# Two feed-forward stages: the expanding matrix products by seven block products in place of eight, with some weight rests and partial sums made by accumulating DMAs

## The chip, the cores and the metric

One core of one Trainium2 chip. The metric is device microseconds (us) from the start of the program to its end. Of the kernel before, three runs give a median of 1385.18 us (1383.61 to 1386.09).

## The reference, cut to what matters

Two transformer blocks run one after the other on 512 tokens of width 1024. Both end in a feed-forward stage, and those two stages are what changes:

```python
# block one: D_FF = 4096
def _sq_relu_mlp(h, w1, w2):
    return jnp.square(jax.nn.relu(h @ w1)) @ w2
...
# block two: D_FF_2 = 2816
x = x + ((jax.nn.silu(h2 @ w_gate[l]) * (h2 @ w_up[l])) @ w_down[l]).astype(x.dtype)
```

So there are three expanding products (w1, here `w_mlp_in`; `w_gate`; `w_up`) and two contracting ones (`w_mlp_out`, `w_down`). All inputs are float32.

## The kernel before, in words

Activations lie transposed: 128 features on the partitions, 512 tokens along the free axis, so a width of 1024 is eight tiles of 128x512.

**Products.** Every float32 matrix is split into a head and a rest in the fp32r format (`hi`, `lo`), and a product is three TensorE products: head by head, head by rest, rest by head (`mm3`, line 619). `dense_tile` (line 791) makes one output tile of 128 features by 512 tokens from all k-tiles of 128: for `w_mlp_in`, `w_gate` and `w_up` that is 8 k-tiles, 24 TensorE products, into one PSUM bank.

**Weights.** `weights` (line 610) loads up to 128x1024 float32 on SyncE's (SP's) queue into a tile of class `raw` (4 buffers), ScalarE casts it to `hi`, and VectorE subtracts to get `lo`. Head and rest take one buffer each of class `w` (10 of them). All of that is per 24 TensorE products in the expanding stages.

**The stages.** `block1` (line 847) makes in turn: the mixer, the product with `w_out`, the residual and norm that give the eight inputs `h2`, and then four parts (`FF1`). A part computes eight tiles of the hidden layer (up), squares them, splits them, and then adds its share to the eight output tiles `y` (down), which stay in SBUF; VectorE adds each part's bank to `y`. `block2` does the same with gate and up together in two parts (`FF2`, 12 and 10 tiles), adding to the residual stream `x`. Between the two parts of the program lie the mixers of block two.

**What sets the order.** The program is first recorded as a list of operations. `Plan.schedule` then issues them one at a time against a table of durations and the state of the buffers, and thereby fixes each engine's order. Nothing is decided at run time: an engine takes its instructions in this order, and each waits for its own inputs. Tile names such as `bank_4348` carry a number that grows with the order in which tiles are first used, so equal numbers on two engines are at about the same place in the program.

Of the kernel before, what the change touches and what calls it, by code (L numbers as in the profile page):

```python
# [67 lines left out]
class Tag:  # L68
    def __init__(self, cls, shape, dtype, cap=None):
        self.cls, self.shape, self.dtype, self.cap = cls, shape, dtype, cap  # L70
        self.needs = [] if cls == "fixed" else [cls] + ([cap[0]] if cap else [])
        self.users = 0
        self.writer = [None, None]
        self.readers = [[], []]
        self.slot = None
        self.real = None
        self.owner = None


class View:  # L80
# [7 lines left out]
    def rows(self, i):  # L88
        v = self[64 * i:64 * i + 64]
        v.parts = (i,)  # L90
        return v
# [89 lines left out]
class Cost:  # L181
# [3 lines left out]
    def __init__(self, eng, fn, args, kw):  # L185
# [5 lines left out]
        elif eng == "SP":  # L191
            self.time = 470
        else:
# [44 lines left out]
class Machine:  # L238
# [38 lines left out]
    def commit(self, c, op, t):  # L277
# [10 lines left out]
        if c.eng == "SP":  # L288
            self.dma = max(self.dma, t + 1150) + op.nbytes / 360.0
            return self.dma + 950  # L290
# [18 lines left out]
class Plan:  # L309
# [13 lines left out]
    def record(self, choices):  # L323
# [12 lines left out]
        op.nbytes = 4 * math.prod(out.shape) if eng == "SP" else 0  # L336
# [144 lines left out]
    def place(self, tag):  # L481
        if tag.real is None:
            self.count += 1
            n = f"{tag.cls}_{self.count}"
            if tag.slot is None:
# [9 lines left out]
    def issue(self, nc, pool, slots, banks):  # L495
        self.pool, self.slots, self.banks, self.count = pool, slots, banks, 0
# [14 lines left out]
FF1 = ((0, 8), (8, 16), (16, 24), (24, 32))  # L511
FF2 = ((0, 12), (12, 22))
SHIFT = 260
LATER = {'mem_norm': 10, 'mem_keys': 100, 'mem_values': 40, 'mod_cols': 140, 'rope_tables': -150, 'late_prologue': 0, 'pool': 90, 'weights': 10, 'lower_bound': 120, 'hgrn': 60, 'add_sq': 120, 'load_raw': 10}
# [5 lines left out]
WIDTH = {"t": 528, "raw": 1024, "w": 1024, "big": 1664, "tmp": 16}  # L520
CAPS = {'t': 54, 'raw': 4, 'w': 10, 'big': 2, 'tmp': 32, 'bank': 8}
# [15 lines left out]
class Builder:  # L537
# [22 lines left out]

    def stat_bank(self, s="st"):
# [28 lines left out]
    def weights(self, src, n, raw=None, engines=None):  # L590
        if raw is None:
            raw = self.load_raw(src, n)
        hi = self.plan.tile("w", [128, 1024], R)
        lo = self.plan.tile("w", [128, 1024], R)
        self.copy(hi[:, :n], raw[:, :n], engines or ("ACT", "POOL"))
        self.tt(ALU.subtract, lo[:, :n], raw[:, :n], hi[:, :n].bitcast(F), engines)
        return hi, lo

# [185 lines left out]
    def chunked(self, w, mt, kts, k0=0):  # L784
        out, o = [], k0
        for kt in kts:
            hi, lo = self.weights(self.a[w][mt, :, o * 128:(o + kt) * 128], kt * 128)
# [13 lines left out]
    def moving(self, w, outs, views, xs):  # L801
        n = len(xs)
        for k in range(n):
            if k % 2 == 0:
                wh, wl = self.weights(self.a[w][k // 2], 1024)
            self.moving_k(wh, wl, k % 2, outs, views, xs[k], k == 0, k == n - 1)

    def build(self):
# [5 lines left out]
        with (  # L814
            tc.tile_pool(name="fixed", bufs=1) as pool,
            tc.tile_pool(name="slots", bufs=1) as sp,
            tc.tile_pool(name="banks", bufs=1, space=PSUM) as pp,
        ):
            with tc.manual_schedule():
                self.plan.issue(nc, pool, sp, pp)  # L820
# [21 lines left out]
    def block1(self):  # L842
# [236 lines left out]
        h2 = []  # L1079
        for k in range(8):  # L1080
            self.residual(k, mo[k], ro)
            h2.append(self.apply_norm(self.x[k], 512, a2[:, k:k + 1], rb, sh2[:, k:k + 1]))
        y, acc = [], None
        self.mem_keys()
        for part, (f0, f1) in enumerate(FF1):
# [6 lines left out]
            for m in range(f0, f1):  # L1092
                b = self.bank("ff")
                self.dense_tile(b, self.chunked("w_mlp_in", m, (8,)), h2)
                r, hi, lo = self.sf("r"), self.sr("ah"), self.sr("al")
                nc.scalar.activation(r, b, AF.Relu)
                nc.scalar.activation(hi, r, AF.Square)
                sq = self.sf("r2")
                self.tt(ALU.mult, sq, r, r)
                self.sub(lo, sq, hi.bitcast(F))  # L1100
                act.append((hi, lo))
            for m in range(8):
                b = self.bank("fo")
                self.dense_tile(b, self.chunked("w_mlp_out", m, (8, 8)[:1] + (f1 - f0 - 8,) * (f1 - f0 > 8), f0), act)
                if part == 0:
                    o = self.sf("y")
                    self.copy(o, b)
                    y.append(o)
                else:
                    nc.vector.tensor_tensor(out=y[m], in0=y[m], in1=b, op=ALU.add)  # L1110
                if part == len(FF1) - 1:
                    acc = self.add_sq(acc, self.square(y[m]))
        self.tail = (y, self.bcast(self.rsqrt(self.stats([acc], 512)[:, :4], 4, 1024), 0, 512), gg2)

# [30 lines left out]
    def pool(self, g, ub):  # L1145
# [3 lines left out]
        u = self.plan.tile("t", [128, 528], F)  # L1149
# [3 lines left out]
        cur, step, n = u, 1, 528  # L1153
        while step < w:
            nxt = self.plan.tile("t", [128, 528], F)
# [136 lines left out]
    def block2(self):  # L1292
# [116 lines left out]
        h = [self.scaled(self.x[k], gn[:, k:k + 1]) for k in range(8)]  # L1409
        rw = self.wide_norm(self.sum_sq(self.x, 512), 512, 1024)  # L1410
        for part, (f0, f1) in enumerate(FF2):
            act = []
            for m in range(f0, f1):
                bg, bu = self.bank("g"), self.bank("u")
                self.dense_tile(bg, self.chunked("w_gate", m, (8,)), h)
                self.dense_tile(bu, self.chunked("w_up", m, (8,)), h)
                sg, p = self.sf("sg"), self.sf("gu")
                nc.vector.tensor_tensor(out=sg, in0=bg, in1=rw, op=ALU.mult)
                nc.scalar.activation(sg, sg, AF.Silu)
                nc.vector.tensor_tensor(out=p, in0=bu, in1=rw, op=ALU.mult)  # L1420
                self.tt(ALU.mult, p, p, sg)
                hi, lo = self.pair(512)
                self.split(p, hi, lo)
                act.append((hi, lo))
            for m in range(8):
                ch = self.chunked("w_down", m, (8, f1 - f0 - 8), f0)
                if part == 0:
# [203 lines left out]

def tile_b(w):
# [50 lines left out]
def host(i):  # L1683
# [44 lines left out]
    d["w_mlp_in"] = tile_a(i["w_mlp_in"][0])  # L1728
# [35 lines left out]
```

## Time and profile before

| | |
|---|---|
| median of the runs | 1385.18 us |
| the profiled execution | 1385.12 us |
| its span, first to last instruction | 1383.3 us |
| TensorE products busy | 1338.9 us, 97% of the span |
| VectorE busy | 846.7 us, 61% |
| ScalarE busy | 571.9 us, 41% |
| GpSimd busy | 38.6 us, 3% |
| DMA, mean | 107 GB/s |

Busy time of an engine is the union of its instructions. TensorE's instructions overlap one another, so the mean duration of one product (some 390 ns for 512 columns) is longer than the spacing from one to the next, and the spacing is what a stretch full of them costs. VectorE's instructions overlap a little at their ends too.

### The profile page before, as it was taken

Reading aid. Unit: us, or ns where it says so; the run is one execution under the profiler, and the core shown is the slowest. Engines: PE = TensorE matmul, PEld = TensorE weight load, DVE = VectorE, ACT = ScalarE, POOL = GpSimd, SP = SyncE. Lnnn points to the kernel's source line nnn. Section 1 sums busy time; section 2 is a strip of 40 time slices with the busy share of each in tenths; the row PEclk is TensorE's granted clock in tenths of the full one; section 3 lists DMA queues with packets and bytes.
Section 4 is the critical chain, followed back from the end, with each engine's and each line's share of the span. In section 5 each row is a group of like instructions: output and inputs, shape, how many; then the busy total and the mean of one; then the engine's idle time right before and its main releaser. Section 6 shows DMA issues by size and latency. Waiting matters only on the chain.

```text
span 1383.3 us, 18475 instructions
## 1 busy us (share of the span) xinstructions
PE 1338.9 (97%) x7202; PEld 1068.7 (77%) x7202; DVE 846.7 (61%) x1544; ACT 571.9 (41%) x952; POOL 38.6 (3%) x58
## 2 busy tenths in 40 slices
PE   6999999999999999999899899999999999999999
PEld 4777777867887888887688677778788888888887
DVE  5787889784453743445845879998864443344432
ACT  4444466544242332334435656667433222232220
POOL 1021120000000000000000000000000000000000
PEclk9999999999999999999899999999999999999999
DMA  9654654232542233323233020211322223332231
GB/s 343 216 138 140 207 186 136 93 105 87 183 151 76 82 102 99 100 92 92 91 91 107 17 66 25 76 46 47 122 76 101 97 69 91 115 107 91 69 101 59
DMA packets 48663, 148.47 MB, mean 107 GB/s; under 512 B 5568, under 2 KB 7232, under 8 KB 48576
## 3 DMA queue, kind: packets, MB, share of 16 engines
q1 hardware_dynamic: 48576, 147.30, 33.4%
q8 instruction: 56, 0.92, 0.3%
q14 instruction: 31, 0.25, 0.1%
HBM read 143.61 MB, written 2.10 MB: 105 GB/s over the span
## 4 chain that ended last, share of the span: by engine, by line
PE 88%; DVE 8%; DMA 2%; issue 1%; ACT 1%; SPq 0%; DVEq 0%; ACTq 0%
PE bank L508 88%; DVE t L508 5%; ACT t L508 1%; DVE tmp L508 1%; DMA raw<-w_mod_b 1%; DVE fixed L508 1%; DVE bank L508 1%; DMA t<-w_mod_a 0%; SPq L508 0%; DMA raw<-w_in_qk 0%; DVE w L508 0%; DVE big L508 0%; ACT w L508 0%; ACT tmp L508 0%; DVEq L508 0%
## 5 line engine op out<-in xcount | busy, mean ns | idle before, releaser
L508 PE MATMUL bank<-t,w 128*128 128x512 f32 (+1 forms) x4716 | 1098.6, 391 | 9.3 <-DVE w L508 4.0
L508 PEld LDWEIGHTS bank<-t,w 128*128 128x128 f32 x4716 | 867.8, 189 | 212.5 <-DVE t L508 6.7
L508 DVE TENSOR_TENSOR w<-raw,w 128x1024 fp32r<-128x1024 f32 (+2 forms) x217 | 250.3, 1158 | 391.4 <-PE bank L508 250.2
L508 ACT CAST w<-raw 128x1024 fp32r<-128x1024 f32 (+2 forms) x214 | 212.0, 994 | 420.2 <-PE bank L508 383.2
L508 DVE TENSOR_TENSOR t<-t,t 128x512 f32<-128x512 f32 (+4 forms) x286 | 167.9, 610 | 35.0 <-ACT t L508 28.0
L508 ACT ACTIVATE t<-t 128x256 f32<-128x256 f32 (+2 forms) x192 | 100.9, 543 | 47.7 <-DVE t L508 32.9
L508 PE MATMUL bank<-t,t 128*64 128x128 f32 (+5 forms) x796 | 92.8, 281 | 6.9 <-DVE t L508 4.3
L508 PEld LDWEIGHTS bank<-t,t 128*128 128x128 f32 (+2 forms) x796 | 73.9, 161 | 23.6 <-DVE t L508 7.7
L508 PE MATMUL bank<-w,t 128*128 128x512 f32 x312 | 76.1, 396 | 0.0
L508 ACT COPY t<-bank 128x512 f32<-128x512 f32 (+3 forms) x93 | 47.9, 518 | 67.7 <-PE bank L508 64.4
L508 ACT ACTIVATE t<-bank 128x512 f32<-128x512 f32 (+2 forms) x74 | 43.4, 587 | 72.6 <-PE bank L508 71.6
L508 PEld LDWEIGHTS bank<-w,t 128*128 128x128 f32 x312 | 57.8, 188 | 15.1 <-ACT t L508 1.3
L508 ACT CAST t<-t 128x512 fp32r<-128x512 f32 (+2 forms) x77 | 44.2, 584 | 55.1 <-DVE t L508 53.5
L508 DVE TENSOR_TENSOR t<-bank,t 128x512 f32<-128x512 f32 (+3 forms) x86 | 56.8, 661 | 8.6 <-PE bank L508 5.4
L508 PE MATMUL bank<-t,fixed 128*32 128x256 f32 (+3 forms) x246 | 38.5, 498 | 13.3 <-DMA t<-w_mod_a 12.3
L508 DVE SCALAR_TENSOR_TENSOR t<-raw,fixed,t 128x512 f32<-128x512 f32 x56 | 43.0, 810 | 12.3 <-DMA raw<-w_mod_b 12.2
L508 PE MATMUL bank<-fixed,t 128*128 128x128 f32 (+2 forms) x292 | 46.8, 279 | 3.4 <-ACT t L508 1.5
L508 PEld LDWEIGHTS bank<-fixed,t 128*128 128x128 f32 x292 | 35.3, 161 | 15.1 <-issue 5.2
L508 DVE TENSOR_TENSOR t<-t 128x512 f32<-128x512 f32 (+1 forms) x68 | 37.9, 557 | 4.5 <-DMA t<-xP 4.1
L508 DVE SCALAR_TENSOR_TENSOR t<-t,fixed,t 128x512 f32<-128x512 f32 (+3 forms) x60 | 38.4, 676 | 1.2 <-ACT t L508 0.9
L508 ACT ACTIVATE t<-bank,fixed 128x512 f32<-128x512 f32 (+2 forms) x32 | 21.8, 682 | 33.2 <-PE bank L508 33.0
L508 PEld LDWEIGHTS bank<-t,fixed 128*32 128x32 f32 (+1 forms) x246 | 13.6, 131 | 27.2 <-ACT fixed L508 12.3
(93 smaller groups left out, 552.8 us busy)
## 6 DMA issues: line engine op xcount, KB each, us to landing
raw<-w_mod_b SPq DMA_DIRECT2D x32, 512.0 KB, 3.9
raw<-w_mlp_in SPq DMA_DIRECT2D x32, 512.0 KB, 3.6
raw<-w_mlp_out SPq DMA_DIRECT2D x32, 512.0 KB, 3.8
raw<-w_in SPq DMA_DIRECT2D x22, 512.0 KB, 3.6
raw<-w_gate SPq DMA_DIRECT2D x22, 512.0 KB, 3.2
raw<-w_up SPq DMA_DIRECT2D x22, 512.0 KB, 3.2
t<-w_mod_a SPq DMA_DIRECT2D x32, 256.0 KB, 6.0
raw<-w_out SPq DMA_DIRECT2D x16, 512.0 KB, 3.8
```

The costliest lines, as they stand in the source:

```text
L508: getattr(engines[eng], fn)(*[real(z) for z in args], **{k: real(z) for k, z in kw.items()})
```

## The change

In the three expanding products an output of 256 features by 512 tokens is now seen as a 2x2 arrangement of blocks (two feature tiles, two halves of 256 tokens), and so is each pair of k-tiles. Seven block products of 256 columns, on sums and differences of weight blocks and of input blocks, take the place of eight. This is the Winograd form of Strassen's method.

- `tile_s` lays these weights out in blocks. `strassen_weights` loads four blocks (128x1024 float32), makes four sums on VectorE (`s1` to `s4`, 256 wide), casts three blocks and the four sums on ScalarE, and makes the two rests: that of the sums (1024 wide) on VectorE; that of the blocks (768 wide) on VectorE for `w_mlp_in`, and for `w_gate` and `w_up` by `rest_dma`: ScalarE writes minus the head, and a DMA that GpSimd issues adds the float32 weights to it from memory.
- `strassen` runs 4 x 7 x 3 = 84 products of 256 columns for two output tiles, into four banks (`quad`). `strassen_sums` puts the result together on ScalarE and VectorE (one copy, two adds of 512, three of 256), `split_quarters` splits it.
- The first two pairs of tiles in block one and the first in block two are made by the ordinary eight (`plain`), while `right_sums` makes the sums of the inputs.
- `weights_dma` loads `w_out`, `w_mem_k`, `w_mem_v` and the plain `w_mlp_in` straight into the head by a DMA that GpSimd issues, and the rest by `rest_dma`.
- The partial sums `y` of block one move to device memory: a part copies its bank and adds it there by an accumulating DMA; the last part reads them back.
- Six parts in block one, four in block two, counted in pairs of tiles. Class `w` now has 5 buffers of twice the width.

```diff
-FF1 = ((0, 8), (8, 16), (16, 24), (24, 32))
-FF2 = ((0, 12), (12, 22))
+FF1 = ((0, 3), (3, 6), (6, 9), (9, 12), (12, 14), (14, 16))
+FF2 = ((0, 3), (3, 6), (6, 9), (9, 11))
+BY_DMA = ("w_out", "w_mem_k", "w_mem_v")
+PLAIN_BY_DMA = ("w_mlp_in",)
+PLAIN1, PLAIN2 = 2, 1
+REST_BY_DMA = ("w_gate", "w_up")
...
-WIDTH = {"t": 528, "raw": 1024, "w": 1024, "big": 1664, "tmp": 16}
-CAPS = {'t': 54, 'raw': 4, 'w': 10, 'big': 2, 'tmp': 32, 'bank': 8}
+WIDTH = {"t": 512, "raw": 1024, "w": 2048, "big": 1664, "tmp": 16}
+CAPS = {'t': 56, 'raw': 4, 'w': 5, 'big': 2, 'tmp': 32, 'bank': 8}
...
+    def weights_dma(self, src, n):
+        hi, lo = self.plan.tile("w", [128, 2048], R).halves()
+        self.nc.gpsimd.dma_start(hi[:, :n], src)
+        self.rest_dma(hi[:, :n], lo[:, :n], src)
+        return hi, lo
...
+    def rest_dma(self, hi, lo, src):
+
+        self.nc.scalar.activation(lo, hi.bitcast(F), AF.Copy, scale=-1.0)
+        self.nc.gpsimd.dma_start(lo, src, accum_op=ALU.add)
...
+    def strassen_weights(self, w, m, u):
+        n, src = 256, self.a[w][m, u]
+        raw = self.load_raw(src, 4 * n)
+        a21, a11, a12, a22 = (raw[:, i * n:(i + 1) * n] for i in range(4))
+        st = self.big(1024)
+        s2, s1, s4, s3 = (st[:, i * n:(i + 1) * n] for i in range(4))
+        self.tt(ALU.subtract, s3, a21, a11)
+        self.tt(ALU.add, s1, a21, a22)
+        self.tt(ALU.add, s2, s3, a22)
+        self.tt(ALU.subtract, s4, a12, s2)
+        (ha, la), (hs, ls) = (self.plan.tile("w", [128, 2048], R).halves() for _ in range(2))
+        self.copy(ha[:, :3 * n], raw[:, n:4 * n], ("ACT",))
+        if w in REST_BY_DMA:
+            self.rest_dma(ha[:, :3 * n], la[:, :3 * n], src[:, n:4 * n])
+        else:
+            self.tt(ALU.subtract, la[:, :3 * n], raw[:, n:4 * n], ha[:, :3 * n].bitcast(F))
+        self.copy(hs, st[:, :4 * n], ("ACT",))
+        self.tt(ALU.subtract, ls, st[:, :4 * n], hs.bitcast(F))
...
+        for k in range(n):
+            for a, b, bank, half in (("a11", "b11", 0, 0), ("a12", "b21", 1, 0), ("a22", "t4", 2, 1), ("s3", "t3", 3, 0),
+                                     ("s1", "t1", 0, 1), ("s2", "t2", 1, 1), ("s4", "b22", 2, 0)):
+                out = quad[bank][:, 256 * half:256 * half + 256]
+                wh, wl = left[k][a]
+                xh, xl = xs[k][b]
+                first = k == 0 and a in ("a11", "a12", "a22", "s3")
+                for i, (w, x) in enumerate(((wh, xh), (wh, xl), (wl, xh))):
+                    t.matmul(out, w, x, start=first and i == 0, stop=k == n - 1 and i == 2, skip_group_check=True)
+        return self.strassen_sums(quad)
...
+    def strassen_sums(self, quad):
+        w, x, y, z = quad
+        s, c, v = self.sf("ps"), self.sf("cu"), self.sf("cd")
+        self.copy(s, w, ("ACT", "DVE"))
+        self.tt(ALU.add, c.rearrange("p (b w) -> p b w", b=2), x.rearrange("p (b w) -> p b w", b=2),
+                s[:, :256].rearrange("p (o w) -> p o w", o=1).to_broadcast([128, 2, 256]))
+        self.tt(ALU.add, v[:, 256:], z[:, :256], c[:, 256:])
+        self.tt(ALU.add, v[:, :256], c[:, 256:], s[:, 256:])
+        self.tt(ALU.add, c[:, 256:], v[:, 256:], s[:, 256:])
+        self.tt(ALU.add, v, y, v)
+        return c, v
...
+                gs, us = self.strassen("w_gate", m, h), self.strassen("w_up", m, h)
+                for g, u, r in zip(gs, us, (rw, rx)):
+                    self.tt(ALU.mult, g, g, r)
+                    nc.scalar.activation(g, g, AF.Silu)
+                    self.tt(ALU.mult, u, u, r)
+                    self.tt(ALU.mult, u, u, g)
+                act += self.split_quarters(*us)
```

Three places show how the engines' orders move.

TensorE at the first crossing from the expanding to the contracting products of block one. Before, the contracting tile `bank_3560` follows `bank_3521`, the eighth expanding tile:

```order
L508 MATMUL bank_3521<-t_3208,w_3312 128x512
L508 MATMUL bank_3521<-t_3216,w_3312 128x512
L508 MATMUL bank_3521<-t_3208,w_3363 128x512
L508 MATMUL bank_3521<-t_3218,w_3312 128x512
L508 MATMUL bank_3521<-t_3228,w_3312 128x512
L508 MATMUL bank_3521<-t_3218,w_3363 128x512
L508 MATMUL bank_3560<-t_3255,w_3340 128x512
```

The split result of that eighth tile is `t_3571`, and `bank_3560` takes it as the last of its eight k-tiles, after 21 products on the seven others.

Of the change, at the crossing of its second part, behind the last expanding bank (`bank_4226`): the contracting tiles are `bank_4348`, `bank_4371` and `bank_4401`, and `t_4385` and `t_4391` are the split result of the last block product:

```order
L519 MATMUL bank_4371<-t_4270,w_4280 128x512
L519 MATMUL bank_4371<-t_4278,w_4280 128x512
L519 MATMUL bank_4371<-t_4270,w_4280 128x512
L519 MATMUL bank_4401<-t_4127,w_4298 128x512
L519 MATMUL bank_4348<-t_4385,w_4183 128x512
L519 MATMUL bank_4371<-t_4385,w_4280 128x512
L519 MATMUL bank_4348<-t_4391,w_4183 128x512
```

Where 21 products of 512 columns stood between the end of the expanding work and the first use of its last result, there are now 25: 12 of `bank_4348`, 12 of `bank_4371` and one of `bank_4401`, which is then left for the two others. In block two there are 28, in the same manner.

VectorE amid gate and up of block two. Before, these rows are the work for one gate tile and one up tile (`w` rows are rests of weights, `t` rows the tail of the tile before):

```order
L508 TENSOR_TENSOR w_10008<-raw_9866,w_9941 128x1024
L508 TENSOR_TENSOR t_10018<-bank_9968,t_9565 128x512
L508 TENSOR_TENSOR w_10042<-raw_9900,w_9975 128x1024
L508 TENSOR_TENSOR t_10052<-bank_10006,t_9565 128x512
L508 TENSOR_TENSOR t_10052<-t_10052,t_10018 128x512
L508 TENSOR_TENSOR t_10066<-t_10052,t_10061 128x512
```

Of the change, a piece of the work for one pair of tiles: sums of weights into `big`, the rest of the sums into `w`, the putting together of one block product (`t_11982`, `t_11990`):

```order
L519 TENSOR_TENSOR big_11922<-raw_11726,big_11922 128x256
L519 COPY t_11955<-bank_11832 128x512
L519 TENSOR_TENSOR w_11948<-big_11911,w_11948 128x1024
L519 TENSOR_TENSOR t_11982<-bank_11841,t_11955 128x512
L519 TENSOR_TENSOR t_11990<-bank_11849,t_11982 128x256
L519 TENSOR_TENSOR t_11990<-t_11982,t_11955 128x256
L519 TENSOR_TENSOR t_11982<-t_11990,t_11955 128x256
L519 TENSOR_TENSOR t_11990<-bank_11845,t_11990 128x512
L519 TENSOR_TENSOR t_11982<-t_11982,t_10763 128x512
L519 TENSOR_TENSOR t_11990<-t_11990,t_10812 128x512
L519 TENSOR_TENSOR t_11982<-t_11982,t_11853 128x512
```

Six instructions per two tiles (twelve per four) have become forty per four, most of them narrower.

ScalarE at the same place: the head of three weight blocks (`CAST` of `w_11837`) and its negative (`ACTIVATE`), which the DMA of GpSimd's queue then completes. The banks `bank_11832` are being filled at this place; `w_11837` is read by the block product after that one, in `bank_11961`:

```order
L519 CAST w_11819<-big_11708 128x1024
L519 CAST w_11837<-raw_11617 128x768
L519 ACTIVATE w_11837<-w_11837 128x768
L519 CAST w_11884<-big_11792 128x1024
L519 ACTIVATE t_11853<-t_11853 128x512
L519 ACTIVATE t_11861<-t_11861 128x512
L519 CAST w_11907<-raw_11671 128x768
L519 ACTIVATE w_11907<-w_11907 128x768
```

GpSimd's queue issued no DMA before. It now issues 112: 16 for `w_out`, 8 each for `w_mem_k`, the plain `w_mlp_in` and `w_mem_v`, 32 for `y`, and 40 for the rests of `w_gate` and `w_up`.

## Rows read from the trace of the kernel before

**Rows 1.** The page, part 1: busy us (share) and instructions of each engine.

```profile
PE 1338.9 (97%) x7202; PEld 1068.7 (77%) x7202; DVE 846.7 (61%) x1544; ACT 571.9 (41%) x952; POOL 38.6 (3%) x58
```

**Rows 2.** The chain that ended last: start us, length us, what.

```profile
291.56 359.40 PE bank L508 x1575
...
965.32 414.76 PE bank L508 x1819
```

**Rows 3.** Busy time by stretch (columns in the first line).

```profile
core 0: us, PE busy (x) PEld busy (x) DVE busy (x) ACT busy (x) POOL busy (x), PEclk, DMA share, GB/s
0.00:68.00 68.00, 54.48 (x333) 40.97 (x334) 42.73 (x89) 30.69 (x58) 6.63 (x18) 1.00 0.80 282
271.00:291.00 20.00, 17.46 (x90) 12.11 (x88) 19.83 (x36) 8.65 (x16) 0.00 (x0) 1.00 0.03 12
291.00:470.00 179.00, 178.44 (x789) 143.70 (x789) 91.02 (x120) 61.80 (x84) 0.00 (x0) 1.00 0.40 125
1100.00:1200.00 100.00, 100.00 (x434) 81.10 (x433) 37.40 (x46) 24.30 (x30) 0.00 (x0) 1.00 0.30 91
1373.20:1380.40 7.20, 6.87 (x59) 6.67 (x57) 1.24 (x3) 0.00 (x0) 0.00 (x0) 1.00 0.15 55
```

**Rows 4.** Timeline of the end, VectorE: start us, us, operation [idle before <-releaser].

```profile
1376.58 0.42 DVE L508 TENSOR_TENSOR t<-fixed,bank 128x256 f32<-128x256 f32 x1 [2.85 <-PE bank L508]
1380.11 0.42 DVE L508 TENSOR_TENSOR t<-fixed,bank 128x256 f32<-128x256 f32 x1 [3.11 <-PE bank L508]
```

**Rows 5.** Groups by shape, VectorE and ScalarE: xcount | busy us, mean ns.

```profile
L508 DVE TENSOR_TENSOR w<-raw,w 128x1024 fp32r<-128x1024 f32 x191 | 234.0, 1228 | 366.4 <-PE bank L508 225.4 <-issue 104.8 <-ACT w L508 36.0
L508 ACT CAST w<-raw 128x1024 fp32r<-128x1024 f32 x189 | 197.7, 1049 | 382.9 <-PE bank L508 345.9 <-DMA raw<-w_mlp_in 9.2 <-issue 7.8
L508 DVE TENSOR_TENSOR t<-t,t 128x512 f32<-128x512 f32 x98 | 65.5, 693 | 9.7 <-ACT t L508 7.2
L508 ACT ACTIVATE t<-t 128x512 f32<-128x512 f32 x80 | 50.6, 633 | 33.7 <-DVE t L508 24.6 <-PE bank L508 4.5 <-DMA t<-xP 3.9
L508 ACT COPY t<-bank 128x512 f32<-128x512 f32 x65 | 37.9, 586 | 60.9 <-PE bank L508 58.7 <-DVE t L508 1.1
L508 DVE TENSOR_TENSOR t<-t,t 128x256 f32<-128x256 f32 x77 | 30.5, 421 | 3.5 <-ACT t L508 2.4
L508 ACT CAST t<-t 128x256 fp32r<-128x256 f32 x13 | 4.8, 406 | 1.5 <-DVE t L508 1.5
L508 DVE TENSOR_TENSOR w<-raw,w 128x768 fp32r<-128x768 f32 x3 | 2.8, 952 | 0.0
L508 ACT CAST w<-raw 128x768 fp32r<-128x768 f32 x3 | 2.5, 836 | 6.5 <-PE bank L508 6.5
```

**Rows 6.** Timeline, VectorE instructions back to back.

```profile
258.33 1.89 DVE L508 TENSOR_TENSOR t<-t,t 128x512 f32<-128x512 f32 x3
...
293.22 2.35 DVE L508 TENSOR_TENSOR w<-raw,w 128x1024 fp32r<-128x1024 f32 x2
```

**Rows 7.** DMA issues: xcount, KB each, median us from issue to landing.

```profile
raw<-w_gate SPq DMA_DIRECT2D x22, 512.0 KB, 3.2
t<-w_mod_a SPq DMA_DIRECT2D x32, 256.0 KB, 6.0
raw<-w_uq SPq DMA_DIRECT2D x3, 384.0 KB, 3.3
```

More of the change, by code (lines that the diff above doesn't have):

```diff
@@ L559, in bank, with quad @@
         return self.plan.tile("bank", [128, 512], F, cap=kind)
+    def quad(self):
+        return [self.plan.tile("bank", [128, 512], F, cap=("x", 8)) for _ in range(4)]
     def stat_bank(self, s="st"):
@@ new lines, in plain @@
+    def plain(self, w, m, xs):
+        outs = [self.bank("ff"), self.bank("ff")]
+        for u in range(2):
+            hi, lo = (self.weights_dma if w in PLAIN_BY_DMA else self.weights)(self.a[w][m, u], 1024)
+            for j in range(2):
+                k = 2 * u + j
+                for block, i, right in ((1, 0, ("b11", "b12")), (0, 1, ("b11", "b12")), (2, 0, ("b21", "b22")), (3, 1, ("b21", "b22"))):
+                    s = slice(block * 256 + j * 128, block * 256 + j * 128 + 128)
+                    first, last = k == 0 and block < 2, k == len(xs) - 1 and block > 1
+                    for c, name in enumerate(right):
+                        t = self.nc.tensor
+                        out = outs[i][:, 256 * c:256 * c + 256]
+                        xh, xl = xs[k][name]
+                        t.matmul(out, hi[:, s], xh, start=first and c == 0, stop=False, skip_group_check=True)
+                        t.matmul(out, hi[:, s], xl, start=False, stop=False, skip_group_check=True)
+                        t.matmul(out, lo[:, s], xh, start=False, stop=last, skip_group_check=True)
+        return outs
@@ new lines, in strassen @@
+    def strassen(self, w, m, xs):
+        t = self.nc.tensor
+        left = [f for u in range(2) for f in self.strassen_weights(w, m, u)]
+        quad = self.quad()
+        n = len(xs)
+        for k in range(n):
[8 more added lines that the diff above has]
+        return self.strassen_sums(quad)
@@ L1092, in block1 @@
             for m in range(f0, f1):
[L1093 to L1101, printed above, removed]
+                if m == PLAIN1:
+                    for z, (e, d) in zip(h2, ed):
+                        self.right_sums(z, e, d)
@@ L1105, in block1 @@
+                if part == len(FF1) - 1:
+                    o = self.sf("y")
+                    nc.sync.dma_start(o, y[m])
+                    nc.vector.tensor_tensor(out=o, in0=o, in1=b, op=ALU.add)
+                    y[m] = o
+                    acc = self.add_sq(acc, self.square(o))
+                    continue
+                o = self.sf("yp")
+                self.copy(o, b)
                 if part == 0:
-                    o = self.sf("y")
-                    self.copy(o, b)
```

183 lines of the change are left out of this document (141 added, 42 removed).

## The prediction

> **What bounds the kernel now.** I read the page's first part, then the chain that ended last, then busy time by stretch. The reader should see that TensorE has work for 97% of the span, VectorE for 61% [rows 1], and that both stages which change are a single piece of TensorE work in the chain: 359.4 us from 291.6 and 414.8 us from 965.3 [rows 2]. (The second piece holds the last products of the mixer too.) Inside them TensorE never rests, while VectorE is busy 91.0 of 179 us and 37.4 of 100 us, and DMA takes 0.40 and 0.30 [rows 3]. The granted clock there is 1.00, its upper level of 2.4 GHz. So fewer columns through TensorE shorten these stages one for one, until another engine or a transfer is late. The forecast asks how much of VectorE's free half the change uses up, and whether its new transfers arrive.
>
> **What TensorE saves.** A product of 512 columns costs its spacing: 100.00 us for 434 [rows 3], 0.2304 us. For 256 columns the end of the kernel has a clean case: the last two banks take 10 k-tiles by 3, so 30 products of 256 columns each, and VectorE, which waits for each bank, starts on them at 1376.58 and 1380.11 [rows 4]: 3.53 / 30 = 0.1177 us. Half the columns cost 51%.
>
> Block one: `w_mlp_in` has 32 tiles by 24 = 768 products of 512 columns, 176.9 us. Now 14 pairs by 84 are 1176, and two ordinary pairs by 96 are 192; 1368 by 0.1177 = 161.0 us. That is 15.9 us less. Block two: gate and up have 44 by 24 = 1056, 243.3 us. Now 10 pairs by 2 by 84 are 1680, and one pair by 2 by 96 is 192; 1872 by 0.1177 = 220.3 us, 23.0 us less. The contracting products keep their number and width. Together **38.9 us**, the most that the stages can give: 1385.1 (the profiled execution, 0.1 below the median of the runs) less 38.9 = 1346.2.
>
> The row that could spoil this is the weight load: in the same stretch loads are busy 6.67 us and products 6.87 us [rows 3], so loads fill TensorE's other half almost wholly, yet run beside the products. The Trainium skill's page "TensorE: Matmul & The Clock Gate" (Part 3, The mechanism) says that a load overlaps products in flight only when the row group differs. By that rule these full-height loads would stand in line with their products, and the sum would be far above today's time (a rival below); the 3.53 us contradict it.
>
> **What the other engines pay.**
>
> *VectorE and ScalarE amid gate and up.* One pair of tiles in block two costs VectorE 16 sums of weights (256 wide), 4 rests (1024), 10 instructions to join the blocks (4 of 512, 6 of 256), 6 multiplications (512) and 4 rests (256): 26 by 0.421, 10 by 0.693, 4 by 1.228 [rows 5] = 22.8 us. TensorE takes 168 by 0.1177 = 19.8 us for it. But means hold overlapped ends: three of 512 in a row take 1.89, so the second and third 0.60 each, and the second of two 1024-wide ones 1.12 [rows 6], some 0.09 less per instruction. With 40 by 0.09 = 3.6 less it is 19.2 us: just under TensorE. The bounds for ten pairs are 0 and 10 by 3.0 = 30 us, less what VectorE prepares in the contracting stretches (a part has 8 by 18 products by 0.2304 = 33.2 us there, against 8 rests of 768 and 8 adds, 13.2 us by means; the five `w` buffers let it make the first product's weights, 5.8 us, ahead). VectorE's own back-to-back rows speak for the low end. I take **4 us**. ScalarE needs some 15 us a pair (8 by 0.836, 4 by 1.049 [rows 5], copies, casts and SiLU) and hides.
>
> *Block one's pairs* cost VectorE 8 by 0.421, 2 by 0.952 and 2 by 1.228 for weights, 2.6 to join, 1.7 to split: 12.0 us by means, 10.4 without overlapped ends, against 9.9 us of TensorE, with contracting stretches between them as above. Only the first part is tight, where the last `right_sums` and `mod_cols` fall as well: bounds 0 and 5, taken **2 us**.
>
> *Start of block one's stage.* Today VectorE is busy 19.83 of 20.00 us there, the chain of residuals and norms [rows 3]. It stays as long: eight rests by shift become four of 512 and eight of 256. What follows it is new: between the last input pair and the last operands of the first block product VectorE has 42 instructions, 25.6 us by means, 21.8 without ends. TensorE has meanwhile some 105 ordinary products and half a block product, 147 by 0.1177 = 17.3 us. The difference is 4.5 us, bounds 0 (some products start late anyway) and 8; taken **4 us**.
>
> *Crossings.* There are ten from expanding to contracting, where there were six. Behind the last bank runs a chain: copy 0.586, two 512-wide adds by 0.69, three 256-wide by 0.421, then in block one ReLU and square 0.633 each, two casts 0.406, a rest 0.421 [rows 5]: 5.7 us plus hand-overs. The cover is 25 by 0.2304 = 5.8 us. In block two four multiplications by 0.69 replace ReLU and square: 7.2 us against 28 by 0.2304 = 6.5 us. Bounds per crossing 0 and 1.6 (one 1024-wide rest and one 256-wide instruction queued ahead on VectorE). I take 0.4 and 0.8: six and four of them, **6 us**.
>
> *Accumulated rests of gate and up.* The trace has no accumulating DMA and none issued by GpSimd. Below: a plain load of 384 KB, 3.3 us; above: twice the slowest plain load, 6.0, at the DMA share of 0.80 at the kernel's start [rows 3], twice because it also reads what it adds to: 12 us [rows 7]. I take 5 us, near the low end, since the share here is 0.30 [rows 3]. The order gives such a buffer out one block product before it is read, 84 by 0.1177 = 9.9 us; ScalarE's cast and negation take 2 by 0.836. So 8.2 us are left, and 5 costs **nothing**. At 12 us each of some 16 products (20 less one at the head of each part) would wait 3.8.
>
> *The other DMAs.* For `w_out`, `w_mem_k`, `w_mem_v` the head's load is now in line with the rest's, on GpSimd's in-order queue, where an issue can stand behind one that waits for a buffer; TensorE is the one that waits there. It has 5.5 us of work per `w_out` chunk and five chunks in flight: nothing, above it one missed chunk of 5 us. The 32 additions to `y` have a whole part (over 60 us) to land; the reads back take no longer than a load. VectorE loses 24 adds to `y`, but ScalarE copies instead; both were covered.
>
> Sum: 1346.2 + 4 + 2 + 4 + 6 = 1362.2. Forecast **1362 us**, in its own range 1350 to 1372.
>
> **The rivals.**
>
> *Everything hides* (0.07): every wait above at its low end, 1346 to 1350. For it: VectorE's 19.2 us are under 19.8. Against it: ten crossings with next to no slack.
>
> *VectorE becomes the bound* (0.18): it pays means, 30 us over ten pairs, of which preparing ahead saves half of 4 by 5.8; 18 us in place of 4, so 1376 (1372 to 1382). For it: in-order waits on ScalarE between its narrow instructions. Against it: the 1.89 us for three.
>
> *Rests land late* (0.11, the other sign): from issue to landing over 8.2 us, TensorE waits in each block product of gate and up. At 10.5 us it is 16 by 2.3 = 37 us, 1399 us. It decides from about 9.6 us, where 16 by 1.4 eats the 23 us between forecast and today. For it: one queue, issued by an engine, reading memory twice over. Against it: 3.2 us for a plain 512 KB [rows 7]. The Trainium skill's page "SBUF — State Buffer" (section SBUF: two separate sides) warns that a DMA issued by GpSimd cannot have its descriptors written while VectorE runs a copy in a two-port mode, and gives 620 ns against 3100 ns. By those figures, as an estimate, 5 us would become 7.5, still within 8.2; no run here shows it yet.
>
> *Narrow products run slower* (0.03, also slower): all of it hangs on 0.1177. The gain of TensorE is nil at (176.9 + 243.3) / 3240 = 0.1297 us, 10% more; at 0.14 the kernel takes 1434. Were each load (6.67 / 57 = 0.117) in line, it would be 3240 by 0.117 = 379 us more, 1741. That is the page's rule above; the end of the kernel has the same three-product pattern and shows 0.1177.
>
> *Given back exactly* (0.04): the costs come to 36 to 42 us, and the time is within 0.2%, 2.8 us, which is about what a measurement of this kernel can tell from no change.
>
> **How the numbers follow.** The forecast's case has 0.57, the rivals 0.07, 0.18, 0.11, 0.03, 0.04. Faster by over 0.2%: 0.57 + 0.07 + 0.18 = 0.82; same 0.04; slower 0.14. The range from 1347 to 1385 leaves out late rests, slow products, half of "everything hides" and the upper half of "same", about 0.19.
>
> **What would show it.** Products of 256 columns in long runs at 0.118 us. The one piece of 359 us in block one gives way to pieces that add up to some 350, the second stage to some 400. At crossings TensorE idles below 1 us, released by VectorE or ScalarE; amid gate and up VectorE is busy over 90%. Landing times of the accumulating DMAs stand in the page's last part: under 8 us I am right on them. The forecast is wrong if TensorE's idle time names a DMA into `w`, if it idles over 10 us amid gate and up with VectorE always busy, or if narrow products are spaced 0.125 us or more.

## The result, and the profile after

The changed kernel takes **1346.92 us** (1345.82 to 1348.84, four runs) against 1384.81 us before: ratio 0.9728, interval 0.9711 to 0.9745. That is 38 us less than before and 15 us less than the forecast of 1362 us: at the lower end, 1347 us, of the whole range, and below the 1350 to 1372 us of the forecast's own case. The profiled execution is 1345.82 us long, its span 1344.0 us.

The page's first part, which answers to [rows 1], and one line of its third part:

```profile
PE 1295.6 (96%) x8600; PEld 1110.0 (83%) x8600; DVE 1047.9 (78%) x2121; ACT 714.8 (53%) x1241; POOL 122.7 (9%) x162
...
q0 software_dynamic: 16128, 45.10, 18.4%
```

TensorE has lost 43 us of busy time; VectorE has 201 us more, ScalarE 143 us. The DMAs that GpSimd issues move 45 MB. The chain that ended last, its pieces in the two stages (compare [rows 2]):

```profile
376.36 221.68 PE bank L519 x1366
...
901.63 237.84 PE bank L519 x1589
1141.96 91.25 PE bank L519 x630
1235.70 81.27 PE bank L519 x546
```

It is still TensorE, cut into pieces. What cuts it in block two stands in TensorE's timeline (start us, us, operation, [idle before <- releaser]):

```profile
1000.06 141.53 PE L519 MATMUL bank<-t,w 128*128 128x256 f32 x1056
...
1141.96 93.36 PE L519 MATMUL bank<-t,w 128*128 128x256 f32 x648 [0.37 <-DVE w L519]
1235.70 87.51 PE L519 MATMUL bank<-t,w 128*128 128x256 f32 x576 [0.37 <-DVE w L519]
1323.96 17.01 PE L519 MATMUL bank<-t,w 128*128 128x512 f32 x84 [0.75 <-ACT t L519]
```

In 344 us TensorE is idle three times, 1.49 us in all. No line names a DMA. Busy time by stretch there, which answers to the 1100 to 1200 row of [rows 3]:

```profile
core 0: us, PE busy (x) PEld busy (x) DVE busy (x) ACT busy (x) POOL busy (x), PEclk, DMA share, GB/s
1010.00:1130.00 120.00, 120.00 (x878) 113.45 (x877) 95.36 (x176) 61.16 (x82) 13.98 (x16) 1.00 0.63 148
1100.00:1200.00 100.00, 99.63 (x703) 92.89 (x702) 81.03 (x149) 51.82 (x72) 11.36 (x13) 1.00 0.64 154
```

The first stretch holds 144 products of 512 columns by form, so (120 - 144 by 0.2304) / 734 = 0.118 us for one of 256: the pace of [rows 4] holds for 120 us on end, with loads busy 113.45 us beside it. VectorE has a fifth of its time left. DMA issues (KB each, median us from issue to landing; compare [rows 7]):

```profile
w<-w_out POOLq DMA_DIRECT2D x16, 512.0 KB, 5.7
dram<-t POOLq DMA_DIRECT2D x32, 256.0 KB, 5.3
w<-w_gate POOLq DMA_DIRECT2D x20, 384.0 KB, 5.7
w<-w_up POOLq DMA_DIRECT2D x20, 384.0 KB, 5.6
```

The accumulating DMAs of gate and up land in 5.7 and 5.6 us. In the two stages, the start of block one's is the one place where TensorE waits long, in the timeline and by stretch:

```profile
305.58 0.72 PE L519 MATMUL bank<-t,w 128*128 128x512 f32 x2 [1.85 <-ACT w L519]
309.16 64.85 PE L519 MATMUL bank<-t,w 128*128 128x256 f32 x386 [2.85 <-DVE w L519]
```

```profile
core 0: us, PE busy (x), PEclk, DMA share, GB/s
305.00:309.00 4.00, 0.72 (x2) 0.95 0.00 0
309.00:317.00 8.00, 7.84 (x42) 0.60 0.43 150
```

It idles 4.70 us, and after that the granted clock is 0.60 for 8 us, mostly the lower level of 1.2 GHz: (1 - 0.60) by 8 + (1 - 0.95) by 4 = 3.4 us more.

**Where the time went.** Three marks cut the span: TensorE's first `fixed,tmp` product in the norm ahead of block one's stage (270.23 before, 267.06 after), its first 128x1 product of block one's final norm (647.56, 637.39), and VectorE's last `fixed<-fixed,bank` add before gate and up (1012.88, 994.02). After, they are these rows of the two timelines:

```profile
267.06 1.16 PE L519 MATMUL bank<-fixed,tmp 128*128 128x128 f32 x8
...
637.39 1.02 PE L519 MATMUL bank<-fixed,t 128*128 128x1 f32 x8
```

```profile
994.02 0.68 DVE L519 TENSOR_TENSOR fixed<-fixed,bank 128x512 f32<-128x512 f32 x1
```

| us | before | after | difference |
|---|---|---|---|
| ahead of block one's stage | 270.2 | 267.1 | -3.2 |
| block one's stage | 377.3 | 370.3 | -7.0 |
| mixers of block two | 365.3 | 356.6 | -8.7 |
| block two's stage | 370.4 | 350.0 | -20.4 |

By TensorE's count block one has -15.9 and block two -23.0 to give. In block one's stretch 13 more products of `w_mem_v` are made early now (27 of form `w,t` against 14, 3.0 us), so it gave 10.0 and the mixers 5.7. A third of what the forecast missed thus lies in mixers that do the same work as before. TensorE alone in block one's stage, before and after (us, PE busy, PEclk, DMA share, GB/s):

```profile
270.23:647.56 377.33, 374.23 (x1648) 1.00 0.34 106
```

```profile
267.06:637.39 370.33, 364.76 (x2270) 0.99 0.58 154
```

It was idle 3.1 us of the stage before (2.5 of them at its start [rows 3]) and is idle 5.6 us after, and it loses 3.4 us at the lower clock, where it lost none. -15.9 + 2.5 + 3.4 = -10.0, which is what the stage gave.

### The profile page after: what moved, and what is told of

Its sections match the earlier page's. It is cut to its first block, busy times and chain, and to the rows that moved or that the text cites. A ratio compares the mean times of both kernels' runs of the same rounds, so it can differ in the third digit from the quotient of the medians.

```text
span 1344.0 us, 22502 instructions
## 1 busy us (share of the span) xinstructions
PE 1295.6 (96%) x8600; PEld 1110.0 (83%) x8600; DVE 1047.9 (78%) x2121; ACT 714.8 (53%) x1241; POOL 122.7 (9%) x162
## 4 chain that ended last, share of the span: by engine, by line
PE 78%; DVE 12%; DMA 5%; issue 2%; ACT 2%; SPq 0%; POOL 0%; DVEq 0%; ACTq 0%; POOLq 0%
PE bank L519 78%; DVE t L519 8%; ACT t L519 2%; DMA t<-w_mod_a 1%; DVE w L519 1%; DMA raw<-w_mod_b 1%; DVE big L519 1%; DMA w<-w_mem_v 1%; DVE tmp L519 1%; DVE fixed L519 0%; DVE bank L519 0%; DMA raw<-w_in_v 0%; DMA t<-xP 0%; DMA raw<-w_mlp_in 0%; ACT w L519 0%
## 5 line engine op out<-in xcount | busy, mean ns | idle before, releaser
L519 PE MATMUL bank<-t,w 128*128 128x256 f32 (+1 forms) x6114 | 1053.9, 332 | 9.1 <-DVE w L519 3.6
L519 ACT CAST w<-raw 128x768 fp32r<-128x768 f32 (+2 forms) x213 | 182.0, 858 | 196.3 <-PE bank L519 148.2
L519 DVE TENSOR_TENSOR t<-t,t 128x512 f32<-128x512 f32 (+4 forms) x510 | 255.3, 538 | 18.1 <-ACT t L519 15.1
L519 DVE TENSOR_TENSOR w<-raw,w 128x768 fp32r<-128x768 f32 (+2 forms) x174 | 172.3, 997 | 47.9 <-ACT w L519 47.4
L519 ACT ACTIVATE t<-t 128x512 f32<-128x512 f32 (+2 forms) x200 | 103.3, 543 | 62.5 <-DVE t L519 44.9
L519 ACT CAST w<-big 128x1024 fp32r<-128x1024 f32 x68 | 71.4, 1050 | 89.3 <-PE bank L519 66.5
L519 DVE TENSOR_TENSOR t<-bank,t 128x512 f32<-128x512 f32 (+4 forms) x148 | 90.7, 614 | 31.9 <-PE bank L519 26.2
L519 ACT CAST t<-t 128x256 fp32r<-128x256 f32 (+1 forms) x193 | 84.5, 478 | 56.6 <-DVE t L519 55.3
L519 DVE TENSOR_TENSOR w<-big,w 128x1024 fp32r<-128x1024 f32 x68 | 83.0, 1221 | 39.6 <-ACT w L519 39.5
L519 DVE TENSOR_TENSOR big<-raw 128x256 f32<-128x256 f32 x136 | 52.9, 422 | 19.8 <-DMA raw<-w_mlp_in 19.2
L519 ACT ACTIVATE w<-w 128x768 fp32r<-128x768 f32 (+1 forms) x60 | 54.8, 916 | 6.5 <-DMA w<-w_mem_k 2.8
```

The source lines that it names most:

```text
L519: getattr(engines[eng], fn)(*[real(z) for z in args], **{k: real(z) for k, z in kw.items()})
```

## The experiments

The theory: TensorE's product count is the gain; VectorE keeps up amid gate and up at its back-to-back spacing; rests arrive in time; the start of block one's stage is the one wait of size; and the mixers' gain is TensorE's clock. Rivals: VectorE or the rests are just at their limit and a part of the gain hangs on a transfer, or the DMAs of weights buy the gain. Every ratio below is to the kernel before on the same chip.

**All pairs ordinary.** No block products; all else as changed, so the ordinary weights of block one come by GpSimd's DMAs throughout (64 of them, where there were 8).

```diff
-PLAIN1, PLAIN2 = 2, 1
+PLAIN1, PLAIN2 = 16, 11
```

> All pairs of tiles made by the ordinary eight block products; the DMA-made weights, the buffers, the parts and the partial sums in memory stay as in the changed kernel. Theory A (TensorE's columns carry the gain): 14 + 2 x 10 = 34 products of a pair each cost 96 - 84 = 12 narrow products more, 34 x 12 x 0.1177 = 48.0 us, less the 8 us of idle time and lower clock at the start of block one's stage, which right_sums causes and which are not there now: 1347 + 48 - 8 = 1387 us, about the kernel before. Theory C (order, buffers and DMAs carry a good part of it): 1375 us or less.

Measured 1397.42 us, ratio 1.0076 (1.0056 to 1.0096): above what each theory said. TensorE's timeline of its stage two:

```profile
1029.54 367.11 PE L519 MATMUL bank<-t,w 128*128 128x256 f32 x2612
```

One piece, no idle. Two products of 256 cost 2 by 0.1177 where one of 512 cost 0.2304, 0.005 more: for 2112 products 2112 by 0.1177 - 243.3 = 5.3 us, and its stage two is 5.2 longer than before (375.6 against 370.4). Against this kernel a seven-block pair saves 96 - 84 = 12 products: 14 pairs in block one and 10 by 2 in block two, 408 by 0.1177 = 48.0 us. The medians differ by 1397.4 - 1346.9 = 50.5, the two ratios by 48.

By stage the count shows in block two: 240 products are 28.2 us, and stage two is 25.6 us shorter in the changed kernel, which waits 1.5 us there. In block one theory A has 14 by 12 by 0.1177 = 19.8, less the 8.1 that the changed kernel loses at the stage's start: 11.7. The profiles differ by 393.9 - 370.3 = 23.6. TensorE's groups from 390 to 630 us, in the kernel with ordinary pairs:

```profile
L519 PE MATMUL bank<-t,w 128*128 128x512 f32 x528 | 133.5, 401 | 0.0
L519 PE MATMUL bank<-t,w 128*128 128x256 f32 x946 | 119.8, 281 | 0.0
```

At their spacings these would take 528 by 0.2304 + 946 by 0.1177 = 233.0 us; they take 240, with no idle time and the clock at 1.00. So this kernel is held up in block one for a reason that is open, and its time overstates what the count is worth there.

**Rests of gate and up on VectorE.**

```diff
-REST_BY_DMA = ("w_gate", "w_up")
+REST_BY_DMA = ()
```

> The rests of gate and up go back to VectorE: four 768-wide subtractions more per pair of tiles, no accumulating DMA there. Theory B (VectorE was at its limit amid gate and up): 19.2 + 4 x 0.87 = 22.7 us a pair against 19.8 us of TensorE, 29 us over ten pairs, of which preparing ahead saves some half: 1347 + 12 to 29 = 1359 to 1376 us. Theory A (it had room, the contracting stretches lend it more): 1345 to 1351 us.

Measured 1355.17 us, ratio 0.9787 (0.9767 to 0.9807), between the two. Stage two takes 357.8 us, 7.8 more than in the changed kernel; the other stretches are within 2 us. TensorE's waits in it, and the stretch of 100 us:

```profile
PE bank L519 <- DVE w L519: 2.8, 6, 0.7
PE bank L519 <- ACT w L519: 1.4, 2, 0.7
...
```

```profile
1100.00:1200.00 100.00, 97.88 (x676) 89.90 (x675) 86.54 (x153) 39.97 (x56) 0.00 (x0) 1.00 0.31 100
```

TensorE's idle time in the stage is 4.0 us more than in the changed kernel; the rest of the 7.8 isn't seen as idle. VectorE is now the one that is late, at the heads of the parts. By the prediction's pricing a pair would cost it 19.2 + 4 by (0.952 - 0.09) = 22.6 us against 19.8: 28 us over ten pairs, less 4 by 5.8 prepared ahead, 5. By means it is 68 - 23 = 45. Measured 7.8, far nearer to the back-to-back spacing with preparing ahead counted in full. The accumulating rests are worth some 8 us.

**Two DMAs per rest.** An accumulating DMA that adds zeros goes ahead of each of the 40.

```diff
+            if "accum_op" in kw and args[0].shape[1] == 768:
+                nc.gpsimd.dma_start(real(args[0]), self.zeros, accum_op=ALU.add)
...
```

> The order is that of the changed kernel, but before each of the 40 accumulating DMAs of gate and up another one adds zeros to the same buffer, and the second waits for the first. From the first issue to the end it takes 2 x 5.7 = 11.4 us. If 8.2 us is all there is, each of some 16 block products waits 3.2 us: 1347 + 51 = 1398 us. If only GpSimd's queue is the limit (two rests of 5.7 us to land per 9.9 us of TensorE): 1.5 us for each of 20, 1347 + 30 = 1377 us. If the order leaves far more room than that: 1352 us or less.

Measured 1446.96 us, ratio 1.0450 (1.0423 to 1.0476), outside every expectation. TensorE's waits, then one of GpSimd's, then the issues:

```profile
PE bank L521 <- DMA w<-w_up: 49.4, 19, 6.3
PE bank L521 <- DMA w<-w_gate: 23.3, 12, 2.9
```

```profile
POOL w L521 <- DMA w<-zeros: 175.3, 28, 8.3
```

```profile
w<-zeros POOLq DMA_DIRECT2D x40, 384.0 KB, 7.0
...
w<-w_gate POOLq DMA_DIRECT2D x20, 384.0 KB, 5.0
w<-w_up POOLq DMA_DIRECT2D x20, 384.0 KB, 5.0
```

The second DMA waits on GpSimd for the first, so a rest takes over 12 us and TensorE waits 72.7 us in 31 spells. Another 27.7 us go to the clock, which stands at the lower level behind some 14 of these spells (the stage cut into slices of 5 us, length by 1 minus granted clock summed; 0.0 in the changed kernel's stage two). 72.7 + 27.7 = 100.4 of the 102.8 us by which stage two is longer. So rests that come late do cost this much, twice what was expected: only some of the products had been counted, and no clock. But the run doesn't tell a rest that lands late from a queue that stands still: GpSimd waits 175.3 us for the zeros, and every later rest stands behind those waits.

**Weights by SP's loads again.** First `w_mem_v` alone (`BY_DMA = ("w_out", "w_mem_k")`), then all of them:

```diff
-BY_DMA = ("w_out", "w_mem_k", "w_mem_v")
-PLAIN_BY_DMA = ("w_mlp_in",)
+BY_DMA = ()
+PLAIN_BY_DMA = ()
```

> Only the weights of mem_v go back to SyncE's load, ScalarE's cast and VectorE's subtraction. Theory C (in the changed kernel these weights come late, so their products fill TensorE's gap between the blocks, and the clock does not fall behind it): the granted clock falls again at the head of block two's mixers and the time is 3 to 6 us longer, 1350 to 1353 us. Rival: it makes no difference, 1346 to 1348 us.

> w_out, w_mem_k, w_mem_v and the ordinary part of w_mlp_in are loaded by SP and get their rests on VectorE or GpSimd again, as before the change; gate and up stay as changed. Theory A: part of the gain comes from there (the stretch ahead of block one is 2.6 us shorter in the changed kernel, and the products of w_mem_v that fill the gap between the blocks are worth 3): VectorE is busy 38.4 of 39 us at the start of block one's stage, and w_out's rests come on top: 1352 to 1357. Rival: these DMAs buy nothing beyond w_mem_v's 3 us: 1349 to 1351.

Measured 1350.29 us, ratio 0.9744 (0.9729 to 0.9758), and 1352.12 us, 0.9755 (0.9741 to 0.9769). The first can't be told from the changed kernel by its interval, and the second's overlaps it only at the end. Without all of these DMAs VectorE is busy 49.91 of 52 us from 268 to 320, and TensorE has two waits for it and one of ScalarE (4.29, 2.35 and 1.67 us) where there were two:

```profile
310.99 1.01 PE L519 MATMUL bank<-t,w 128*128 128x256 f32 x3 [4.29 <-DVE w L519]
313.67 64.62 PE L519 MATMUL bank<-t,w 128*128 128x256 f32 x385 [1.67 <-ACT w L519]
```

In both, the last `w_mem_v` products wait for VectorE in the gap between the blocks (2.50 and 2.44 us) as before the change, and there the clock falls. The second of them by stretch, TensorE alone (us, PE busy, PEclk, DMA share, GB/s):

```profile
664.00:672.00 8.00, 8.00 (x26) 0.57 0.71 218
```

So in the traces these DMAs help at the two gaps, by some 3 to 5 us; by the runs it is not clear of noise, for both ratios also lie within the interval of the changed kernel's later runs (0.9711 to 0.9763, below). The early gain of 3.2 us does not come from these DMAs: this kernel reaches the first mark at 265.48. Nor does it come from the clock, which falls twice ahead of the first mark in the changed kernel's profile (3.4 us lost) and not at all before.

**The clock in the mixers.** For each profile, the mixers' length and the time lost at the lower level in them (the same sum over slices of 5 us):

| kernel | mixers, us | lost by the clock, us | rest |
|---|---|---|---|
| before | 365.3 | 13.6 | 351.7 |
| changed | 356.6 | 5.1 | 351.5 |
| changed, profiled again | 358.9 | 8.6 | 350.3 |
| `w_mem_v` by SP | 363.6 | 10.3 | 353.3 |
| all weights by SP | 363.6 | 11.9 | 351.8 |
| rests on VectorE | 358.1 | 6.8 | 351.3 |

Before, the places are 669 to 679 us, 765 to 771, 836 to 840 and 901 to 908. The first, around the idle spell, in the timeline of before:

```profile
671.87 1.22 PE L508 MATMUL bank<-t,w 128*128 128x512 f32 x2 [3.99 <-DVE w L508]
```

In seven of the eight other profiles the rest is 349 to 352 us, and 356.3 in one that moves work into the mixers (the short first part, below). So nearly all of the 8.7 us is time at the lower level that fell away. (The 3.0 us of moved work hardly show in the rest: TensorE is idle 19.3 us in the mixers, where it was idle 17.4.) Part of that is luck: of thirteen profiles behind the change the changed kernel's first lost the least (5.1 to 11.9 us, median 8.5), and its second lost 8.6. In the gap between the blocks, next to the wait for `w_mem_v`'s rests (21 to 27 us behind the mark at the end of block one's stage), the clock falls before and in both kernels that load `w_mem_v` by SP, and in no other. But in seven of the eleven other profiles it falls 0 to 9 us behind that mark instead, so without that wait it often falls all the same. At the other places the runs don't settle why it came less often.

**The start of block one's stage.** A third ordinary pair, or a first part of the two ordinary pairs alone:

```diff
-PLAIN1, PLAIN2 = 2, 1
+PLAIN1, PLAIN2 = 3, 1
```

```diff
-FF1 = ((0, 3), (3, 6), (6, 9), (9, 12), (12, 14), (14, 16))
+FF1 = ((0, 2), (2, 5), (5, 8), (8, 11), (11, 14), (14, 16))
```

> The third input pair of block one stays ordinary, so the sums of the right side are due one pair later; TensorE has 96 - 84 = 12 products of 256 columns more, 1.4 us. Theory A: the two idle spells at the stage's start (1.85 and 2.85 us in the changed kernel) and the stretch at the lower clock behind them (3.4 us) belong to the sums being late, and both go: 1347 - 8.1 + 1.4 = about 1340. Rival B: the sums only become late at the next place, the head of part two, and the time stays at 1346 to 1349. Rival C: the idle goes but the clock falls at another place: about 1344.

> Block one's first part has only the two ordinary pairs; the other 14 pairs lie in parts of 3, 3, 3, 3 and 2. TensorE's products keep their number, and the sums of the right side are due one contracting stretch later (8 by 12 by 0.2304 = 22.1 us). Theory A: what TensorE loses at the stage's start (4.7 us idle, 3.4 us by the clock) goes and nothing takes its place: about 1339. Rival B: a short idle spell at the crossing out of part one takes its place, as with three ordinary pairs (2.1 us idle, then 1.7 us at the lower clock): about 1343. Rival C: no difference from the changed kernel beyond 2 us.

> The changed kernel itself once more, beside the three that follow, so that differences of a few microseconds are read on one chip: 1345 to 1349 is expected by every theory.

Three ordinary pairs: 1346.13 us, ratio 0.9703 (0.9685 to 0.9721). Two alone: 1345.39 us (1344.64 to 1345.84), 0.9706 (0.9685 to 0.9727). The changed kernel once more: 1349.22 us (1345.10 to 1353.78), 0.9737 (0.9711 to 0.9763), just above the 1345 to 1349 expected. With two alone the stage takes 362.5 us in place of 370.3 and 371.0; 11 of the `w_mem_v` products moved out of it, 2.5 us, so 5.3 to 6.0 were gained, and the clock does not fall there:

```profile
335.41 0.74 PE L519 MATMUL bank<-t,w 128*128 128x256 f32 x4 [0.87 <-ACT w L519]
...
346.80 260.00 PE L519 MATMUL bank<-t,w 128*128 128x256 f32 x1627 [0.69 <-ACT w L519]
```

Four short waits of 2.6 us in all are left of 4.7 + 3.4. That is theory A in the stage; but the mixers take 364.9 us, 6 to 8 more. 2.5 of that is the moved work, and 3.4 is clock against the first profile of the changed kernel, none against the second; the rest is open. With three pairs the wait moved to the crossing, as rival B had it:

```profile
370.01 0.99 PE L519 MATMUL bank<-fixed,t 128*128 128x128 f32 x4 [2.10 <-ACT t L519]
```

Both may be 1 to 4 us faster than the changed kernel; the intervals overlap, and it is not shown.

**Rests of block one by DMA too**, alone and with the short first part:

```diff
-REST_BY_DMA = ("w_gate", "w_up")
+REST_BY_DMA = ("w_gate", "w_up", "w_mlp_in")
```

> Block one's left blocks get their rests by accumulating DMAs as gate and up do: VectorE sheds 28 rests of 768 columns (0.95 us each, 26.6 us), ScalarE gets 28 negations, GpSimd 28 more issues. Theory A: VectorE's share of the start stall shrinks by the one or two rests that stand ahead of the first block product, 1 to 2 us, and nothing else changes: 1344 to 1347. Rival B: the 28 issues of 0.8 us hold up the sums into y and the loads behind them in GpSimd's queue, and TensorE waits for DMAs: over 1350.

> Both: a first part of two ordinary pairs, and block one's rests by accumulating DMAs. If each theory A holds, VectorE is off the path at the stage's start: 1337 to 1340. If the idle spell moves to the crossing: 1341 to 1344. If GpSimd's queue becomes late: over 1347.

Measured 1358.71 us, ratio 0.9807 (0.9783 to 0.9832), and 1355.15 us, 0.9784 (0.9757 to 0.9810): slower by 9 and 6 us than the changed kernel on the same chip, though VectorE has 27 us less to do. In the first of the two the loss is largest near the end of the stage, where `y` is read back and additions to `y`, loads and rests fall together. By stretch (all engines, as in [rows 3]; DMA's share counts a packet where it starts, so it can exceed 1):

```profile
578.00:592.00 14.00, 12.67 (x61) 10.30 (x59) 3.53 (x8) 7.10 (x10) 4.37 (x6) 1.00 1.06 253
```

and VectorE waits there for the load of the next weights, then TensorE for VectorE:

```profile
588.56 0.76 DVE L519 TENSOR_TENSOR big<-raw 128x256 f32<-128x256 f32 x2 [5.29 <-DMA raw<-w_mlp_in]
```

```profile
593.94 12.72 PE L519 MATMUL bank<-t,w 128*128 128x256 f32 x82 [2.11 <-DVE w L519]
```

All DMA engines are busy. The three loads of `w_mlp_in` issued there take 9.4, 11.4 and 13.5 us to land, against 7.6, 9.4 and 11.4 in the changed kernel, which has a share of 1.04 at this place and just gets by. GpSimd is busy only 4.37 of these 14 us, so it is the transfers that are late and not its issues: rival B was right on the time, but wrong on the cause. That reading rests on one profile. With the short first part the longest wait lies elsewhere, at the crossing out of that part, with the clock at 0.57 over the 8 us from 344:

```profile
345.37 80.56 PE L519 MATMUL bank<-t,w 128*128 128x256 f32 x518 [4.82 <-ACT w L519]
```

**Three and five parts in block two.**

```diff
-FF2 = ((0, 3), (3, 6), (6, 9), (9, 11))
+FF2 = ((0, 4), (4, 8), (8, 11))
```

and `((0, 2), (2, 4), (4, 6), (6, 8), (8, 11))`.

> Gate and up in three parts of 4, 4 and 3 pairs where there are four: one crossing less, 8 sums into x less on VectorE, and one contracting stretch less in which VectorE can prepare weights. Theory A: VectorE keeps up with TensorE amid gate and up (its spacing, 19.2 us per pair against 19.8), and crossings cost under 0.8 us: 1346 to 1348. Rival B: VectorE pays its means (22.8 us per pair) and lives on what it prepares in the contracting stretches; one stretch less costs up to 5.8 us: 1350 to 1353.

> Gate and up in five parts of 2, 2, 2, 2 and 3 pairs: one crossing more, and behind four of the five only one earlier pair of tiles is ready when the last pair leaves its banks. Theory A: crossings are cheap as in the changed kernel (0.37 to 0.75 us): 1347 to 1349. Rival B: a crossing is covered only by products of tiles that are ready, 4 banks by 2 tiles by 3 = 24 by 0.2304 = 5.5 us against a chain of 7.2 us, so 1.7 us at four crossings less the 0.4 that they cost now: about 1352.

Measured 1351.70 us, ratio 0.9745 (0.9724 to 0.9766), and 1353.13 us, 0.9757 (0.9740 to 0.9775). The totals fit the rivals, but runs of the changed kernel on the same chip reach from 1345.10 to 1353.78, and the stages don't fit: stage two takes 351.2 and 352.6 us where the changed kernel has 350.0. With five parts TensorE's waits in it are

```profile
PE bank L519 <- ACT t L519: 3.0, 4, 0.8
```

0.75 us at each of four crossings, half of rival B's 1.7. Of the profiled spans the other 5.4 and 2.0 us lie ahead of the stage, at places that these edits don't touch. The clock makes 3.4 of the first; of the second it makes nothing in sum (1.7 more in the mixers, 1.7 less ahead of block one's stage).

## Why the prediction was right, and where it was off

The frame held: TensorE bounds the kernel before and after, and 38.9 us of its products went. The time was 15 us below the forecast. It lies at the lower end of the range, where the rival "Everything hides" stood (1346 to 1350 us, chance 0.07), but not for that rival's reason: the waits and the clock cost 5.9 us in block one's stage, and time outside the two stages gave 8.9 back. That the time came out near 1346.2, the sum without any cost, is thus in part luck. Step by step, against the profiled span:

- **What TensorE saves**, 38.9: right. The pace of 0.1177 us holds, and the comparison with ordinary pairs gives 27.1 (25.6 and 1.5 of waits) for 28.2 in block two. The rule on weight loads of the Trainium skill's page "TensorE: Matmul & The Clock Gate" (Part 3, The mechanism), by which a load overlaps products in flight only when the row group differs, is contradicted by this trace: full-height loads are busy 113.45 of 120 us in which TensorE never rests. (The same section also has loads pulled ahead into a background weight buffer, which fits.)
- **VectorE amid gate and up**, 4: measured 0.74, two waits of 0.37. The mechanism is the right one, as the kernel with all rests on VectorE shows, which is 8 us past the limit; the size was off since VectorE had a fifth of its time left. The forecast of over 90% busy there was wrong: 81%.
- **Block one's first part**, 2: nothing shows, apart from the next point.
- **Start of block one's stage**, 4: 4.7 of idle, in two waits, for a ScalarE head and a VectorE rest. The step left out two things. TensorE was idle 2.5 us there before, too, so the stage's idle time rose by 2.5 only; and the clock falls behind the waits, another 3.4 us: 5.9 in all. A shorter first part takes away 5.3 to 6.0 us, which shows the cause.
- **Crossings**, 6: mis-sized. 0.75 us for block two and 0.8 (0.45 and 0.34) for block one, 1.5 in all: at the others the chain was covered. With five parts in block two, where fewer tiles are ready, it is 0.75 at each of four.
- **Accumulated rests**, 0 with 5 us to land: 5.6 and 5.7, and no wait. By the Trainium skill's page "SBUF — State Buffer" (section SBUF: two separate sides) the estimate was 7.5; no such delay shows, but VectorE ran only two-input TENSOR_TENSOR instructions and four copies out of banks in the 120 us from 1010, so the trace hardly tests what the page says of copies. The rival's decision point, some 8 to 10 us, was not tried; at over 12 us (two DMAs per rest) TensorE waits as the rival has it, and the price was too low by the clock.
- **Other DMAs**, 0: right for TensorE's waits. But they help fill the place where `y` is read back, to a share of 1.04; with 28 more rests by DMA the kernel was 9 us slower.
- **What the sum left out**: it took the time outside the stages as unchanged. The mixers lost 8.7 us, 5.7 of it not moved work, and the early part 3.2. The first goes with time at the lower clock, some 3 of it by luck of this profile; the second was not separated.

Sum of the difference: block one gave 10.0 where -15.9 + 2 + 4 + 2.4 = -7.5 was forecast, block two 20.4 where 15.8 was, the mixers 5.7 and the early part 3.2 where nothing was: 2.5 + 4.6 + 5.7 + 3.2 = 16.0, and the profiled execution lies 16.4 below the forecast (the crossings' 5.6 stood as 6 in its sum).

## What to carry to other kernels

Price a second engine's load by its back-to-back spacing, and credit what it prepares in stretches where it rests: that came out at 5 us for 7.8 measured, where means gave 45. When TensorE bounds a kernel, look behind each of its idle spells for a fall of the granted clock (4.7 us of idle and 3.4 of clock here), in stages that a change doesn't touch as well; subtract what was idle before, and expect a few microseconds of this to differ from run to run. And look at DMA's share at the place where streams meet, not at its mean: 0.64 amid gate and up cost TensorE nothing, while at 1.04, at the reading back of `y`, there was no room for more.

## What the runs showed of the hardware

An accumulating DMA of 384 KB, issued by GpSimd, lands in 5.0 to 5.7 us against 3.3 for a plain load of that size on SP's queue [rows 7]. Its issue holds GpSimd for 0.87 us, and one that must wait holds the queue (28 waits, 175.3 us, with two DMAs per rest). The granted clock fell behind single idle spells of 1.7 to 4 us, but not behind each: 0.60 over the 8 us behind 1.85 and 2.85 us here, no fall behind 1.70 us at 643.79 in the same profile, while the kernel with three ordinary pairs fell behind a spell of the same length at that place. A short fall costs 1.7 us (0.76 over 7 us there), and one kernel's mixers lost 5.1 and 8.6 us to such falls in two profiles; the changed kernel's runs on one chip spread over 1345.10 to 1353.78.
